# A hybrid decoder layer on one core: the rotation moves to VectorE, e's blocks later, scores in single banks, division on ScalarE

## The chip, the core and the metric

The kernel runs on one core of a Trainium2 chip. The core has a matrix engine (TensorE, PE in the profile), a vector engine (VectorE, DVE), an engine for activations (ScalarE, ACT), a general-purpose one (GpSimd, POOL) and SyncE (SP), which only issues transfers. Each works through its own queue in order and waits on semaphores for the others. Matrix products land in PSUM, which has eight banks of 2 KB a partition; everything else lives in SBUF. The metric is the device time of one execution in microseconds, the median over runs.

## The reference

One layer on a sequence of 512 tokens with 2048 features, all in 32-bit floats:

```
h = rms_norm(x, norm_gain);  z = h @ w_in
q, k, v, g_attn, c_b, c_c, c_h, g_conv = split(z)
q, k = partial_rope(rms_norm(q)), partial_rope(rms_norm(k))   # first 16 of 64 columns of a head turn
y_attn = sliding_window_attention(q, k, v, sinks) * silu(g_attn)
y_conv = c_b * short_conv(c_c * c_h) * silu(g_conv)
x = x + concat(y_attn, y_conv) @ w_out
gate = sigmoid(rms_norm(x) @ w_ple_gate + b)
e = rms_norm(p @ w_ple_proj)
x = x + gate * e
```

There are 16 query heads and 4 key heads of 64 columns. Attention looks back 128 tokens, so a block of 128 queries sees two blocks of keys (the first block sees one). The softmax has a learned sink in its denominator: probabilities are exp(scores - m) divided by (their sum + exp(sink - m)).

## The kernel before, in words

Each fp32 operand is split in two: a high half rounded to TensorE's fast 32-bit format (wh, hsh, made by a cast on ScalarE, L199) and the rest (wl, hsl, by a subtraction on VectorE, L200). A product is three matmuls, high by high, low by high, high by low. Large products are done in groups of 1024 output columns by a scheme of seven products of half blocks in place of eight, which is what `steps` lists; a step is 12 matmuls of 512 columns. `run_step` prepares the weights two steps ahead.

There are three parts. The first makes the keys, values and group 0 (the queries). The second, which most of the change touches, does what doesn't fit into groups. TensorE's queue is there written out by hand: `gemm_tile` runs 16 pairs of three matmuls (L701) for seven tiles of the short convolution's inputs, and after every second pair `tick` lets one piece of other work into the queue: transposes of keys (`make_k`), four blocks of `e_block` and sixteen units of `attention`, each for one key head j and one block n of 128 queries. `at(when, fn)` sets the tick. A unit turns its queries (`turn_q`, three ticks before), makes four heads' scores (L790, L791) into PSUM, takes the row minimum and mask on VectorE (L796), the exponential on ScalarE (L801), turns the probabilities (L816, five ticks later), splits them and multiplies by the values (L826, L827, two ticks after that). The other four engines' order in this part is set by a scheduler, from the order of the code and its own costs. In the first and third parts it is the order of the code.

An `e_block` multiplies p by 512 columns of w_ple_proj: 24 matmuls (L867) into four banks, one for each block of tokens. `take_e` then squares a bank on ScalarE with a row sum (L858), multiplies it by the gain on VectorE (L860) and stores it through GpSimd's queue (L861). Two of the four banks are the pair that attention's scores use (`ps_s`, one buffer of two banks), two are those of the turned probabilities (`ps_t`).

The rotation (`rope`) runs on GpSimd: four products with tables, one difference and one sum (L407 to L409), for each of four key blocks and four half-sets of queries. Query set (t, n) holds token blocks 2t and 2t+1 and heads 8n to 8n+7. Sets (0, 1) and (1, 1) are scaled and turned at the start of the second part, (0, 0) and (1, 0) inside it. Its scratch tile and most other short-lived tiles of this part come from one pool, `misc`, of eight buffers.

The third part runs groups 1 to 8. Group 4 is the attention's gate: its quarters z get silu (L992) on ScalarE; `normalise` (L1074) multiplies them on VectorE by `rs`, the reciprocals of the softmax sums; then TensorE turns them (L986) and VectorE multiplies the attention rows by them (L1083).

## Time and profile before

| | |
|---|---|
| median of 3 runs | 944.35 us (944.24 to 945.08) |
| profiled execution | 943.3 us, its span 941.5 us |
| TensorE busy | 915.0 us, 97% of the span |
| VectorE busy | 729.7 us, 78% |
| ScalarE busy | 532.5 us, 57% |
| GpSimd busy | 176.0 us, 19% |
| mean granted TensorE clock | 0.991 |
| second part | from 127.03 us; first scores at 184.95 us; last tile of the part at 294.35 us |

The span runs from the first to the last instruction; the execution's own time lies 1.8 us over it. A row of a timeline gives the start, the time to the end of the last of its instructions, the engine, the line, what is written from what, the shapes and, in brackets, how long the engine had been idle before and who ended that. Matmuls overlap, so the time between two starts says what one costs, not its own duration. A row of a group gives busy time in all, the mean of one in nanoseconds, and the idle time before them. In the row of a window the engines' busy times are followed by the TensorE clock that was granted as a share of full speed, the share of time that the transfer engines were busy, and GB/s.

### The profile page before, as it was taken

Reading aid. Unit: us, or ns where it says so; the run is one execution under the profiler, and the core shown is the slowest. Engines: PE = TensorE matmul, PEld = TensorE weight load, DVE = VectorE, ACT = ScalarE, POOL = GpSimd, SP = SyncE. Lnnn points to the kernel's source line nnn. Section 1 sums busy time; section 2 is a strip of 40 time slices with the busy share of each in tenths; the row PEclk is TensorE's granted clock in tenths of the full one; section 3 lists DMA queues with packets and bytes.
Section 4 is the critical chain, followed back from the end, with each engine's and each line's share of the span. In section 5 each row is a group of like instructions: output and inputs, shape, how many; then the busy total and the mean of one; then the engine's idle time right before and its main releaser. Section 6 shows DMA issues by size and latency. Waiting matters only on the chain.

```text
span 941.5 us, 12095 instructions
## 1 busy us (share of the span) xinstructions
PE 915.0 (97%) x4202; PEld 758.0 (81%) x4202; DVE 729.7 (78%) x1038; ACT 532.5 (57%) x855; POOL 176.0 (19%) x248
## 2 busy tenths in 40 slices
PE   9999997889999999999999999899999999999997
PEld 7888876678788888888888888788888888888885
DVE  5877976777873876877667768989678696999778
ACT  6767836477873443446344446455566676575453
POOL 4232196512222000100100120010221112001100
PEclk9999998999999999999999999999999999999999
DMA  8999434523557877435925887785997995578747
GB/s 296 361 291 325 164 109 165 196 79 79 101 95 198 311 222 233 121 112 173 239 80 160 275 215 234 224 219 139 261 332 223 225 287 158 135 226 271 185 134 213
DMA packets 69086, 189.83 MB, mean 202 GB/s; under 512 B 8097, under 2 KB 14561, under 8 KB 69025
## 3 DMA queue, kind: packets, MB, share of 16 engines
q1 hardware_dynamic: 47520, 131.09, 40.4%
q0 software_dynamic: 21360, 57.96, 27.5%
q8 instruction: 33, 0.54, 0.2%
q14 instruction: 29, 0.23, 0.1%
q10 hardware_dynamic: 144, 0.01, 0.0%
HBM read 159.67 MB, written 29.36 MB: 201 GB/s over the span
## 4 chain that ended last, share of the span: by engine, by line
PE 65%; DVE 3%; issue 1%; ACT 0%; DVEq 0%
PE psp L241 58%; PE pst L241 3%; PE pst L986 2%; PE pst L1339 1%; PE psg L701 1%; DVE wl L200 1%; DVE z L1239 1%; DVE wy L189 1%; DVE z L1074 0%; DVE form L200 0%; ACT z L992 0%; DVE z L1293 0%; DVE z L1224 0%; DVE z L1221 0%; DVE z L323 0%
## 5 line engine op out<-in xcount | busy, mean ns | idle before, releaser
L241 PE MATMUL psp<-wh,form 128*128 128x512 f32 x1280 | 395.2, 390 | 0.0
L241 PEld LDWEIGHTS psp<-wh,form 128*128 128x128 f32 x1280 | 239.3, 188 | 49.1
L241 PE MATMUL psp<-wl,form 128*128 128x512 f32 x640 | 249.2, 389 | 0.0
L200 DVE TENSOR_TENSOR wl<-wy,wh 128x1024 fp32r<-128x1024 f32 x108 | 131.7, 1222 | 53.7 <-ACT wh L199 53.0
L199 ACT CAST wh<-wy 128x1024 fp32r<-128x1024 f32 x108 | 113.5, 1051 | 101.2 <-PE psp L241 70.4
L241 PEld LDWEIGHTS psp<-wl,form 128*128 128x128 f32 x640 | 120.2, 188 | 25.0
L200 DVE TENSOR_TENSOR wl<-wx,wh 128x1024 fp32r<-128x1024 f32 x72 | 88.0, 1223 | 51.2 <-ACT wh L199 51.1
L241 PE MATMUL psp<-wh,hsh 128*128 128x512 f32 x304 | 119.3, 392 | 0.0
L241 PE MATMUL psp<-wh,hsl 128*128 128x512 f32 x304 | 118.7, 391 | 0.0
L241 PE MATMUL psp<-wl,hsh 128*128 128x512 f32 x304 | 118.7, 390 | 0.0
L199 ACT CAST wh<-wx 128x1024 fp32r<-128x1024 f32 x72 | 75.6, 1053 | 75.5 <-PE psp L241 51.9
L199 ACT CAST wh<-ws 128x1024 fp32r<-128x1024 f32 x72 | 75.9, 1054 | 73.7 <-PE psp L241 51.6
L200 DVE TENSOR_TENSOR wl<-ws,wh 128x1024 fp32r<-128x1024 f32 x72 | 88.1, 1223 | 28.6 <-ACT wh L199 28.5
L189 DVE TENSOR_TENSOR wy<-wy,ws 128x1024 f32<-128x1024 f32 x72 | 87.7, 1218 | 0.0
L241 PEld LDWEIGHTS psp<-wl,hsh 128*128 128x128 f32 x304 | 57.3, 189 | 12.2
L241 PEld LDWEIGHTS psp<-wh,hsh 128*128 128x128 f32 x304 | 57.4, 189 | 11.8
L241 PEld LDWEIGHTS psp<-wh,hsl 128*128 128x128 f32 x304 | 57.4, 189 | 11.8
L169 POOL DMA_DIRECT2D wy<-in_w_mid x16 | 14.1, 880 | 200.1 <-DVE wy L189 154.2
L701 PE MATMUL psg<-hsh,wh 128*128 128x512 f32 x112 | 46.3, 413 | 0.0
L200 DVE TENSOR_TENSOR wl<-raw,wh 128x1024 fp32r<-128x1024 f32 (+1 forms) x29 | 34.5, 1190 | 14.9 <-ACT wh L199 14.8
L701 PE MATMUL psg<-hsh,wl 128*128 128x512 f32 x112 | 44.0, 393 | 0.0
L701 PE MATMUL psg<-hsl,wh 128*128 128x512 f32 x112 | 43.8, 391 | 0.0
(217 smaller groups left out, 1345.0 us busy)
## 6 DMA issues: line engine op xcount, KB each, us to landing
ws<-in_w_mid SPq DMA_DIRECT2D x40, 512.0 KB, 4.3
wx<-in_w_mid SPq DMA_DIRECT2D x24, 512.0 KB, 3.6
wy<-in_w_mid SPq DMA_DIRECT2D x20, 512.0 KB, 5.3
h<-form POOLq DMA_DIRECT2D x32, 256.0 KB, 5.8
wy<-in_w_mid POOLq DMA_DIRECT2D x16, 512.0 KB, 8.5
raw<-in_w_in SPq DMA_DIRECT2D x16, 512.0 KB, 3.8
wx<-in_w_out SPq DMA_DIRECT2D x16, 512.0 KB, 6.7
ws<-in_w_out SPq DMA_DIRECT2D x16, 512.0 KB, 5.2
```

What stands on the lines that cost most here:

```text
L169: nc.gpsimd.dma_start(t, w[n, r, j, c], accum_op=ALU.add)
L189: tt(y, y, got[g, "s1" if f == 6 else "s0", c], op=ALU.add)
L199: nc.scalar.copy(h, src)
L200: tt(l, src, f32(h), op=ALU.subtract)
L241: nc.tensor.matmul(ps[t], a, w[:, i], start=start and first and i == 0 and n == 0, stop=last and i == 1 and n == 2, skip_group_check=not s ...
L701: nc.tensor.matmul(ps, w[:, k % 8], a, start=k == 0 and n == 0, stop=k == KT - 1 and n == 2)
L986: nc.tensor.transpose(pt[:, b], quads[b // 2][:, b % 2, f * P : (f + 1) * P], ident)
L1239: stt(z[:, b, cols], z[:, b, cols], column(r_e, t, b), ext[t, n][b][:, cols], op0=ALU.mult, op1=ALU.mult)
L1339: nc.tensor.matmul(ps, w[:, k % 8], a, start=k == 0 and n == 0, stop=k == KT - 1 and n == 2)
```

## The change

Four edits and some that follow from them.

- `rope` runs on VectorE (`tt`) and in two products over 16 columns in place of four over 8: the tables `turns` hold cosine and sine in the order in which each product takes them. Scratch tiles come from `misc` in the second part.
- The four blocks of e stand later in TensorE's queue: before the ninth, 17th, 21st and 25th pair of `gemm_tile` in place of the fifth, ninth, 17th and 21st. Each bank is taken after its own matmuls, and the first bank no longer waits for the second. The weights are loaded in the new order. `misc` has nine buffers.
- `ps_s` has two buffers of one bank each in place of one of two. A unit's four heads of scores use two tiles, which come free apart.
- In the gate, three of the four quarters are multiplied by `rs` on ScalarE, 8 activations of 64 columns at a time (one head of one token block each), in two halves at different steps. The last quarter stays on VectorE.
- The second half-sets of queries are squared, scaled and rotated at ticks 13 to 20 in place of 2 to 8. Two small constants are loaded first.

```diff
--- before.py
+++ after.py
...
@@ -389,24 +389,24 @@
     nc.gpsimd.tensor_tensor(kq_g, kq[:, 0:1], kq[:, 1:2], op=ALU.mult)
 
     half = ROT // 2
-    turns = [const.tile([P, 4, NB, half], F32, name=f"turn{i}") for i in range(2)]
+    turns = [const.tile([P, 2, NB, ROT], F32, name=f"turn{i}") for i in range(2)]
     for i in range(2):
-        for n, (what, part_) in enumerate(((0, 0), (1, 1), (0, 1), (1, 0))):
-            gain = rope_g[:, i, part_ * half : (part_ + 1) * half].unsqueeze(1).broadcast_to([P, NB, half])
-            nc.gpsimd.tensor_tensor(turns[i][:, n], trig[:, what], gain, op=ALU.mult)
-
-    work_tile = [itile]
-    def rope(z, which, blocks):
+        for n in range(2):
+            for p in range(2):
+                gain = rope_g[:, i, p * half : (p + 1) * half].unsqueeze(1).broadcast_to([P, NB, half])
+                nc.gpsimd.tensor_tensor(
+                    turns[i][:, n, :, p * half : (p + 1) * half], trig[:, (n + p) % 2], gain, op=ALU.mult
+                )
+
+    def rope(z, which, blocks, junk):
 
         nb, nh = z.shape[1], z.shape[2]
-        lo, hi = z[:, :, :, :half], z[:, :, :, half : ROT]
-        t = work_tile[0]("rope")[:, : 4 * nb * nh * half].rearrange("p (n b h d) -> p n b h d", n=4, b=nb, h=nh)
-        for n, src in enumerate((lo, hi, hi, lo)):
-            w = turns[which][:, n, blocks].unsqueeze(2).broadcast_to([P, nb, nh, half])
-            nc.gpsimd.tensor_tensor(t[:, n], src, w, op=ALU.mult)
-        nc.gpsimd.tensor_tensor(lo, t[:, 0], t[:, 1], op=ALU.subtract)
-        nc.gpsimd.tensor_tensor(hi, t[:, 2], t[:, 3], op=ALU.add)
+        t = junk("rope")[:, : 2 * nb * nh * ROT].rearrange("p (n b h d) -> p n b h d", n=2, b=nb, h=nh)
+        for n in range(2):
+            w = turns[which][:, n, blocks].unsqueeze(2).broadcast_to([P, nb, nh, ROT])
+            tt(t[:, n], z[:, :, :, :ROT], w, op=ALU.mult)
+        tt(z[:, :, :, :half], t[:, 0, :, :, :half], t[:, 0, :, :, half:], op=ALU.subtract)
+        tt(z[:, :, :, half:ROT], t[:, 1, :, :, :half], t[:, 1, :, :, half:], op=ALU.add)
 
 
     hs, kv_split = [], []
@@ -560,7 +560,7 @@
 
     def scale_k(b):
         tt(k_of(b), k_of(b), msk[:, b].unsqueeze(2).broadcast_to([P, NKV, HD]), op=ALU.mult)
-        rope(kv[b][:, : NKV * HD].rearrange("p (o h d) -> p o h d", o=1, d=HD), 1, slice(b, b + 1))
+        rope(kv[b][:, : NKV * HD].rearrange("p (o h d) -> p o h d", o=1, d=HD), 1, slice(b, b + 1), mtile)
 
     def q_of(t, n):
         return qs[t, n].rearrange("p b (h d) -> p b h d", d=HD)
@@ -578,7 +578,7 @@
             for b in range(2):
                 tt(z[:, b], z[:, b], ms[:, b].unsqueeze(2).broadcast_to([P, 8, HD]), op=ALU.mult)
 
-        return squares, lambda: head_rstd(ms, rx2_tok[:, blocks]), scale, lambda: rope(z, 0, blocks)
+        return squares, lambda: head_rstd(ms, rx2_tok[:, blocks]), scale, lambda: rope(z, 0, blocks, mtile)
 
     quarters(0, qs, 0)
     soon(after, 0, evict_kv)
@@ -587,8 +587,8 @@
     for j, s in enumerate((6, 6, 7, 7, 9, 9, 10, 10)):
         soon(after, s, form7, j)
 
-    jobs = [io["w_in"][TCC, 0], io["w_ple_proj"][0], io["w_ple_proj"][1], io["w_in"][TCC, 1], io["w_ple_proj"][2],
-            io["w_in"][TCH, 0], io["w_ple_proj"][3], io["w_in"][TCH, 1]]
+    jobs = [io["w_in"][TCC, 0], io["w_ple_proj"][0], io["w_in"][TCC, 1], io["w_ple_proj"][1],
+            io["w_in"][TCH, 0], io["w_ple_proj"][2], io["w_ple_proj"][3], io["w_in"][TCH, 1]]
     for i in range(1, 4):
         jobs += [io["w_in"][t + i, c] for t in (TCC, TCH) for c in range(2)]
     raws, splits, job = {}, {}, [0]
@@ -660,10 +660,10 @@
-    misc = second.enter_context(tc.tile_pool(name="misc", bufs=8, side="right", reuse_waits="tile"))
+    misc = second.enter_context(tc.tile_pool(name="misc", bufs=9, side="right", reuse_waits="tile"))
-    ps_s = second.enter_context(tc.tile_pool(name="ps_s", bufs=1, space=PSUM, reuse_waits="tile"))
+    ps_s = second.enter_context(tc.tile_pool(name="ps_s", bufs=2, space=PSUM, reuse_waits="tile"))
@@ -720,9 +719,9 @@
     scale_q(1, 1)
     for t in range(2):
         for b in range(2):
-            at(2 + t, lambda t=t, b=b: square_q(t, 0, b, mtile))
-        at(3 + t, lambda t=t: q_then[t, 0][0]())
-        at(7 + t, lambda t=t: scale_q(t, 0))
+            at(13 + t, lambda t=t, b=b: square_q(t, 0, b, mtile))
+        at(14 + t, lambda t=t: q_then[t, 0][0]())
+        at(19 + t, lambda t=t: scale_q(t, 0))
     mask = cw.tile([P, 2 * P], F32, name="mask", bufs=1)
     nc.gpsimd.dma_start(mask, io["mask"])
     vv = vvp.tile([P, NB, NKV, 2, HD], F32R, name="vv")
@@ -783,18 +782,19 @@
                 tt(st[oth, :, hf], pt[own], f32(st[own, :, hf]), op=ALU.subtract)
 
         def scores():
-            sc = ps_s.tile([P, 4, 2 * P], F32, name="pss")
+            sc = [ps_s.tile([P, 2, 2 * P], F32, name="pss") for _ in range(2)]
             ks = slice(n * P + lo - P, (n + 1) * P)
             for r in range(4):
                 q = cell["q"][:, r // 2, r % 2]
-                nc.tensor.matmul(sc[:, r, lo:], q, khh[j][:, ks], start=True, stop=False)
-                nc.tensor.matmul(sc[:, r, lo:], q, kll[j][:, ks], start=False, stop=True)
+                out = sc[r // 2][:, r % 2, lo:]
+                nc.tensor.matmul(out, q, khh[j][:, ks], start=True, stop=False)
+                nc.tensor.matmul(out, q, kll[j][:, ks], start=False, stop=True)
             t = ap.tile([P, 4, 2 * P], F32, name="prob")
             negm, sums, sk = (small.tile([P, 4], F32, name=x) for x in ("negm", "sums", "sk"))
             for r in range(4):
                 h = 4 * j + r
                 nc.vector.tensor_tensor_reduce(
-                    t[:, r, lo:], sc[:, r, lo:], mask[:, lo:], -(HD**-0.5), nsink[:, h : h + 1],
+                    t[:, r, lo:], sc[r // 2][:, r % 2, lo:], mask[:, lo:], -(HD**-0.5), nsink[:, h : h + 1],
                     ALU.add, ALU.min, negm[:, r : r + 1],
                 )
             for r in range(4):
@@ -850,8 +850,8 @@
         if n < 3:
             load_pg(n + 1)
         ws = next_job()
-        pair = ps_s.tile([P, 4, 2 * P], F32, name="pss").rearrange("p (t a) b -> p t (a b)", t=2)
-        banks = [pair[:, 0], pair[:, 1]] + [ps_t.tile([P, T], F32, name="pst") for _ in range(2)]
+        banks = [flat(ps_s.tile([P, 2, 2 * P], F32, name="pss")) for _ in range(2)]
+        banks += [ps_t.tile([P, T], F32, name="pst") for _ in range(2)]
 
         def take_e(t):
             e = mtile("e")
@@ -865,14 +865,14 @@
                 h, l = (a[:, k, t * P : (t + 1) * P] for a in pts)
                 for i, (a, w) in enumerate(((h, ws[0]), (l, ws[0]), (h, ws[1]))):
                     nc.tensor.matmul(banks[t], a, w[:, k], start=k == 0 and i == 0, stop=k == 1 and i == 2)
-            for i in {1: (0, 1), 2: (2,), 3: (3,)}.get(t, ()):
+            for i in (t,):
                 take_e(i)
 
     load_pg(0)
     order = [(j, n) for j in (2, 3, 0, 1) for n in range(NB)]
     for u, (j, n) in enumerate(order):
         attention(j, n, 13 + 34 * u // 15)
-    mids = {0: {4: lambda: e_block(0), 8: lambda: e_block(1)}, 1: {0: lambda: e_block(2), 4: lambda: e_block(3)}}
+    mids = {0: {8: lambda: e_block(0)}, 1: {k: lambda n=n: e_block(n) for n, k in ((1, 0), (2, 4), (3, 8))}}
 
 
     for i in range(4):
@@ -1062,21 +1062,28 @@
         s0, q = g * PER, {}
         quarters(g, q, s0)
         soon(after, s0 + 17, lambda: silu(q[0, 1], 0))
-        soon(after, s0 + 18, lambda: normalise(0, 1))
+        soon(after, s0 + 18, lambda: normalise(0, 1, 0))
+        soon(after, s0 + 19, lambda: normalise(0, 1, 1))
         soon(after, s0 + 21, lambda: silu(q[1, 1], 1))
-        soon(after, s0 + 22, lambda: normalise(1, 1))
+        soon(after, s0 + 21, lambda: normalise(1, 1, 0))
+        soon(after, s0 + 22, lambda: normalise(1, 1, 1))
         soon(after, s0 + 26, lambda: silu(q[0, 0], 0))
-        soon(after, s0 + 27, lambda: normalise(0, 0))
-
-        def normalise(t, n):
+        soon(after, s0 + 26, lambda: normalise(0, 0, 0))
+        soon(after, s0 + 27, lambda: normalise(0, 0, 1))
+
+        def normalise(t, n, h):
+
             for b in range(2):
-                z = q[t, n][:, b].rearrange("p (h d) -> p h d", d=HD)
-                tt(z, z, rs[:, 2 * t + b, 8 * n : 8 * n + 8].unsqueeze(2).broadcast_to([P, 8, HD]), op=ALU.mult)
+                for i in range(4 * h, 4 * h + 4):
+                    z = q[t, n][:, b, i * HD : (i + 1) * HD]
+                    nc.scalar.activation(z, z, AF.Copy, scale=rs[:, 2 * t + b, 8 * n + i : 8 * n + i + 1])
 
         def last():
             q[1, 0] = qtile("z")
             silu(q[1, 0], 1, psum[g, "a"])
-            normalise(1, 0)
+            for b in range(2):
+                z = q[1, 0][:, b].rearrange("p (h d) -> p h d", d=HD)
+                tt(z, z, rs[:, 2 + b, 0:8].unsqueeze(2).broadcast_to([P, 8, HD]), op=ALU.mult)
 
         def times(j):
             raw = pairs[id(mixf), j][0]
```

Where the scheduler and the code put the instructions now can be seen at three places. First VectorE at the start of the second part, before:

```order
L200 TENSOR_TENSOR wl<-raw,wh 128x1024
L710 COPY rb<-rx_tok 128x512
L562 TENSOR_TENSOR kv<-kv,msk 128x256 x4
L556 TENSOR_TENSOR msq<-msq,r_x 128x16 x2
L200 TENSOR_TENSOR wl<-raw,wh 128x1024
L579 TENSOR_TENSOR z<-z,msq 128x512 x4
L200 TENSOR_TENSOR wl<-raw,wh 128x1024
```

Here wl is the low half of the convolution's first weights, of e's first weights and of the convolution's second ones, kv a key and value block, msk and msq the heads' scales, z a query set. With the change the last rows ahead of the same cast of e's first weights, and that cast:

```order
L556 TENSOR_TENSOR msq<-msq,r_x 128x16 x2
L408 TENSOR_TENSOR kv<-rope 128x4x8
L409 TENSOR_TENSOR kv<-rope 128x4x8
L579 TENSOR_TENSOR z<-z,msq 128x512 x3
L407 TENSOR_TENSOR rope<-z,turn_225 128x256 x2
L579 TENSOR_TENSOR z<-z,msq 128x512
L408 TENSOR_TENSOR z<-rope 128x16x8
L409 TENSOR_TENSOR z<-rope 128x16x8
L407 TENSOR_TENSOR rope<-z,turn_225 128x256 x2
L200 TENSOR_TENSOR wl<-raw,wh 128x1024
```

In between stand the other rotations and scalings of the four key blocks. The cast of e's first weights moved behind all rotations of keys and one and a half of queries; it stood ahead of all of them.

Second VectorE from the second unit's last reduction to the third's first one. Before:

```order
L796 ISA negm 128x1
L887 TENSOR_TENSOR u<-psg,zc 128x512
L805 TENSOR_TENSOR sk<-attn_sinks,negm 128x4
L783 TENSOR_TENSOR st<-psm,st 64x2x128
L807 TENSOR_TENSOR sums<-sums,sk 128x4
L808 RECIPROCAL rs<-sums 128x4
L891 SCALAR_TENSOR_TENSOR yconv<-u,conv_w,yconv 128x512
L783 TENSOR_TENSOR st<-psm,st 64x2x128
L891 SCALAR_TENSOR_TENSOR yconv<-u,conv_w,yconv 128x512
L200 TENSOR_TENSOR wl<-raw,wh 128x1024
L796 ISA prob,negm<-pss,mask,nsink 128x256
```

and now:

```order
L796 ISA negm 128x1
L887 TENSOR_TENSOR u<-psg,zc 128x512
L805 TENSOR_TENSOR sk<-attn_sinks,negm 128x4
L556 TENSOR_TENSOR msq<-msq,r_x 128x16 x2
L200 TENSOR_TENSOR wl<-raw,wh 128x1024
L807 TENSOR_TENSOR sums<-sums,sk 128x4
L782 TENSOR_TENSOR st<-psm,st 64x2x128
L808 RECIPROCAL rs<-sums 128x4
L891 SCALAR_TENSOR_TENSOR yconv<-u,conv_w,yconv 128x512
L782 TENSOR_TENSOR st<-psm,st 64x2x128
L891 SCALAR_TENSOR_TENSOR yconv<-u,conv_w,yconv 128x512
L796 ISA prob,negm<-pss,mask,nsink 128x256
```

prob and negm are a head's masked scores and their row minimum, u and yconv the convolution's, st the turned queries. Two products of msq came in: the scales of the other query sets, which GpSimd's power has to give first; the cast wl moved ahead of the evictions st. Above and below these rows stand also four sums of squares (L548), four scalings (L579) and two rotations of those sets.

Third ScalarE in the gate, from the second quarter's silu (L992) on. Before:

```order
L992 ACTIVATE z<-z,r_x 128x512 x2
L199 CAST form<-raw 128x256
L199 CAST form<-g 128x256
L199 CAST wh<-wy 128x1024
L199 CAST form<-g 128x512
L199 CAST form<-g 128x256
L199 CAST wh<-ws_5409 128x1024
L199 CAST form<-raw 128x512
```

and now:

```order
L992 ACTIVATE z<-z,r_x 128x512 x2
L1079 ACTIVATE z<-z,rs 128x64 x8
L199 CAST form<-raw 128x256
L199 CAST form<-g 128x256
L199 CAST wh<-wy 128x1024
L1079 ACTIVATE z<-z,rs 128x64 x8
L199 CAST form<-g 128x512
L199 CAST form<-g 128x256
L199 CAST wh<-ws_5419 128x1024
L199 CAST form<-raw 128x512
```

wh is the high half of a step's weights, form that of an input block. Two groups of eight activations (L1079) stand now before the two weight casts that follow the silu.

5 lines of the change are left out of this document (2 added, 3 removed).

## The prediction

> **What bounds the kernel now.** I read the page's first lines, then the list of waits on TensorE, then the windows and the timeline of the stretches that the waits point to.
>
> ```profile
> span 941.5 us, 12095 instructions
> PE 915.0 (97%) x4202; PEld 758.0 (81%) x4202; DVE 729.7 (78%) x1038; ACT 532.5 (57%) x855; POOL 176.0 (19%) x248
> PE pss L867 <- DVE e L860: 11.8, 3, 6.0
> PE pss L790 <- DVE negm L796: 3.7, 3, 2.5
> PE pst L986 <- DVE z L1074: 2.4, 2, 2.1
> ```
>
> TensorE has work for 97% of the span, so the most that any schedule can win is the 26.5 us without it (941.5 - 915.0) and what its clock loses. The list says where most of it lies: three waits in the blocks of e (L867), three at the scores (L790), two at the transposes of group 4 (L986). All other TensorE work is untouched by the change. In the windows (engine busy times, then the granted clock, DMA share and GB/s) the clock stands behind the engines:
>
> ```profile
> 127.03:184.95 57.92, 46.15 (x191) 37.01 (x190) 37.91 (x62) 29.16 (x59) 39.49 (x67) 0.91 0.48 162
> 184.95:294.35 109.40, 105.07 (x584) 87.49 (x583) 81.06 (x256) 77.77 (x231) 29.53 (x36) 1.00 0.48 104
> 604.42:615.10 10.68, 8.27 (x34) 6.61 (x32) 10.68 (x15) 4.62 (x8) 1.14 (x2) 0.84 0.79 210
> 145.00:150.00 5.00, 4.99 (x12) 3.93 (x13) 2.90 (x5) 3.84 (x9) 2.58 (x2) 0.50 0.20 75
> 173.40:177.40 4.00, 3.98 (x11) 3.15 (x12) 2.10 (x4) 0.87 (x4) 1.63 (x3) 0.57 0.93 316
> 199.60:203.00 3.40, 3.37 (x21) 3.00 (x22) 1.75 (x6) 2.30 (x8) 0.00 (x0) 1.00 0.32 118
> 607.50:611.00 3.50, 3.48 (x11) 2.98 (x12) 3.50 (x5) 0.00 (x0) 0.00 (x0) 0.53 0.88 178
> ```
>
> After some waits the clock is halved (0.50, 0.57, 0.53), after another it isn't (1.00 from 199.60 on). The timeline of TensorE gives the waits themselves, and the chain of waits an undisturbed run of matmuls:
>
> ```profile
> 145.01 0.79 PE L867 MATMUL pss<-wh,ptsh 128*128 128x512 f32 x1 [6.01 <-DVE e L860]
> 160.35 0.50 PE L867 MATMUL pss<-wh,ptsh 128*128 128x512 f32 x1 [1.37 <-DVE e L860]
> 173.42 0.50 PE L867 MATMUL pss<-wh,ptsh 128*128 128x512 f32 x1 [4.39 <-DVE e L860]
> 184.95 0.22 PE L790 MATMUL pss<-khh,st 128*128 128x128 f32 x1
> 294.35 10.88 PE pst L1339 x48
> ```
>
> An undisturbed 128x512 matmul takes 0.227 us (48 in 10.88), at half clock about twice that, so the e stage costs more than its 11.8 us of waits. From 127.03, the first matmul of the convolution part, to the first score at 184.95 are 57.92 us. TensorE issues there 174 matmuls (78 of L701, 96 of L867) at 0.227, 39.5 us, and 16 small transposes at about 0.09, 1.4 us: 40.9. **17.0 us** of the stretch are waits and half clock.
>
> **Who makes e wait.** GpSimd does the rotation, and e's consumers stand behind it:
>
> ```profile
> L407 POOL TENSOR_TENSOR rope<-kv,turn 128x32 f32<-128x32 f32 x16 | 9.3, 610 | 0.3 <-DVE kv L562 0.3
> 127.03 6.32 POOL L407 TENSOR_TENSOR rope<-kv,turn 128x32 f32<-128x32 f32 x4 [0.29 <-DVE kv L562]
> 143.05 0.45 POOL L409 TENSOR_TENSOR z<-rope 128x128 f32<-128x128 f32 x1
> 140.96 0.69 DVE L860 TENSOR_TENSOR e<-pss,pg 128x512 f32<-128x512 f32 x1 [3.91 <-POOL z L409]
> ```
>
> The four k rotations and the first two of q hold GpSimd from 127.03 to 143.50; VectorE's first product of e waits 3.91 us for it, and TensorE's second block, whose banks those products free, waits 6.01. The products' stores also go through GpSimd:
>
> ```profile
> e<-e POOLq DMA_DIRECT2D x16, 256.0 KB, 2.9
> ```
>
> **The change, part by part.** (a) *Rotation on VectorE.* The prices come from VectorE's own rows at this place:
>
> ```profile
> 126.47 1.42 DVE L562 TENSOR_TENSOR kv<-kv,msk 128x256 f32<-128x256 f32 x4
> 127.81 0.33 DVE L556 TENSOR_TENSOR msq<-msq,r_x 128x16 f32<-128x16 f32 x2
> 128.06 1.21 DVE L200 TENSOR_TENSOR wl<-raw,wh 128x1024 fp32r<-128x1024 f32 x1
> 129.19 2.48 DVE L579 TENSOR_TENSOR z<-z,msq 128x512 f32<-128x512 f32 x4
> 131.60 1.21 DVE L200 TENSOR_TENSOR wl<-raw,wh 128x1024 fp32r<-128x1024 f32 x1
> ```
>
> From start to start these give 0.335 us for 256 columns, 0.125 for 16, 1.13 for 1024, 0.60 for 512. The rotation of k is 8 products of 64 columns and 8 sums of 32. No row has these sizes: at least 0.125 each, at most 0.335. I take 0.14 and 0.125, since the cost follows the columns: 2.1 us in place of GpSimd's 11. The two rotations of q are 4 products of 256 columns (1.34) and 4 sums of 128 (about 0.2 each). VectorE does them ahead of the low half of e's first weights. By the new order, from 126.47: four scalings of k 1.34, rotation 2.1, small ones 0.25, four scalings of q 2.4, four products 1.34, two sums 0.4, so that cast starts at 134.3 and lands 1.2 later, 135.5. TensorE gets there by 24 matmuls and 8 transposes, 5.45 + 0.72 after 127.03, and two matmuls: 133.65. A **new wait of 1.9 us**, between 1.6 (all small ones at 0.125) and 5.4 (all at 0.335).
>
> (b) *e's blocks later, taken part by part.* Blocks 1 to 3 come after the rotations. Between two blocks lie 12 or more matmuls, so a bank is asked for again some 7 us after its last matmul. TensorE fills a bank in 6 x 0.227 = 1.36, and VectorE's product of it takes 0.69, so the consumers keep its pace; if a store's landing (2.9) holds a buffer, the ninth one and the 7 us cover it, and without that cover a wait is like today's smallest, 1.37. I count no wait for blocks 1 to 3. The stage becomes 40.9 + 1.9 = 42.8, a **gain of 15.1 us** (11.6 with the long rotation, 15.4 with the short); the first score moves to 169.8.
>
> (c) *Scores in single banks, q's second half later.* The scores can follow after two of four reductions instead of four. But the squares, norms and rotations of the other half of q now stand among the first units of attention:
>
> ```profile
> 199.63 0.35 PE L790 MATMUL pss<-khh,st 128*128 128x256 f32 x1 [2.51 <-DVE negm L796]
> L548 DVE TENSOR_REDUCE msq<-sqq 128x8 f32<-128x512 f32 x8 | 5.3, 680 | 2.5 <-ACT sqq L547 2.5
> L796 DVE CUSTOM_DVE_ANT_0 prob<-pss,mask,nsink 128x256 f32<-128x256 f32 x48 | 20.3, 480 | 3.3 <-PE pst L816 3.1
> L305 POOL TENSOR_TENSOR msq<-msq,half_neg 128x16 f32<-128x16 f32 x4 | 12.6, 3140 | 4.4 <-DVE msq L300 4.4
> ```
>
> By the new order VectorE does, between the end of the first scores (170.7) and the third unit's reductions: the rest of e 0.4, four sums of squares 2.4, reductions 1.1 + 1.6, the evictions of q 4 x 0.35, u 0.6, a cast 1.13, two steps of the convolution 1.4, small ones 1.1. Before the cast it must also wait for two powers on GpSimd in a row at 3.14 us, which start near 174.6: 180.9. After them the cast, two evictions, two steps and small ones, 3.4, so the reductions start at 184.3 and two are done at 185.1. TensorE is ready for the fourth unit's scores at 181.7: a wait of 3.4 where 2.51 stands now. The four scalings (2.4) and two rotations (2 x 1.08) that come next push the fourth unit's work and the low halves of the second's probabilities, about 2 us of TensorE. With 0.7 for half clock and small waits I count 6.3 for the stage against 4.3 now (109.40 - 105.07 in its window): a **loss of 2.0**. Bounds: a gain of 4.3 if the early release takes all waits away, a loss of 9.6 if the added work passes to TensorE whole (2.4 + 2.4 + 2.2 + 0.9, and 1.7 for the powers).
>
> The Trainium skill, "TensorE: Matmul & The Clock Gate", Part 1, halves the clock after an idle window of about 3.4 us, free-running. The rows agree for 4.39 and 2.51, not for 607, where two waits of 2.12 and 0.30 sufficed. By it the 3.4 us wait is a toss-up, and the sum would be 0.7 less or 0.7 more.
>
> (d) *Division in the gate on ScalarE.* TensorE's rows at the transposes of group 4, then VectorE's and ScalarE's:
>
> ```profile
> 604.42 0.38 PE L986 MATMUL pst<-ident,z 128*128 128x128 f32 x2
> 606.92 0.30 PE L986 MATMUL pst<-ident,z 128*128 128x128 f32 x1 [2.12 <-DVE z L1074]
> 607.52 1.30 PE L986 MATMUL pst<-ident,z 128*128 128x128 f32 x5 [0.30 <-DVE z L1074]
> 615.10 1.03 PE L986 MATMUL pst<-ident,z 128*128 128x128 f32 x8
> 590.34 1.29 DVE L1074 TENSOR_TENSOR z<-z,rs 128x512 f32<-128x512 f32 x2
> 606.09 1.28 DVE L1074 TENSOR_TENSOR z<-z,rs 128x512 f32<-128x512 f32 x2
> 600.67 1.34 ACT L992 ACTIVATE z<-z,r_x 128x512 f32<-128x512 f32 x2 [3.35 <-DVE z L323]
> L801 ACT ACTIVATE prob<-prob,negm 128x128 f32<-128x128 f32 x16 | 6.2, 393 | 4.5 <-DVE negm L796 4.5
> L806 ACT ACTIVATE sk<-sk 128x4 f32<-128x4 f32 x16 | 3.2, 198 | 0.0
> ```
>
> From 604.42 to 615.10 TensorE does 8 transposes (0.87) and 24 matmuls (5.44); 4.4 us are lost to the wait for L1074 and half clock. VectorE is busy through the whole window (10.68 of 10.68), so the two pairs that leave it, 1.2 each, bring its queue 2.4 forward. ScalarE gets 48 activations of 64 columns with a per-row factor, 8 at a time, between the weight casts. Their rows lie between 0.20 (128x4) and 0.39 (128x128 with a per-row bias), 0.29 in the middle; two of L992 take 1.34 from start to end at some 0.72 each, so starts lie 0.1 closer than the durations. I take 0.21, 1.7 us for eight. The eight for the first transposes then end near 603, ahead of 604.42. Two eights delay the casts by 3.4 before the weights of the next two steps are due. So a **gain of 2.3**, what VectorE gives up; between -0.7 and 4.4.
>
> (e) Constants, loads of weights in another order, GpSimd's freed time: nothing. The constants are due at 127, over 100 us after they land, and each weight load still stands two jobs ahead of its cast. If that cover went, one load, 3.8 us to land.
>
> Sum: 941.5 - 15.1 + 2.0 - 2.3 = 926.1. The profiled execution took 943.3 for a span of 941.5, and the median is 944.35, 2.85 over the span: 926.1 + 2.85 = **929.0 us**.
>
> **The rivals.** *VectorE's queue in attention.* The loss of (c) at its upper bound, 9.6 instead of 2.0: 936.6. For it: the powers stand in VectorE's queue as waits. Against: it idles a fourth of the stage now. 17%.
>
> *e still waits.* Blocks 1 to 3 and the first scores each find a bank late by the smallest of today's waits, 1.37: 5.5 more, 934.5. For it: every product's buffer waits for a store. Against: the rotation that made it is gone. 13%.
>
> *Activations at the price of the row above, 0.39.* Eight take 3.1, the casts come 2.8 later than counted, (d) loses 0.7: 932.0. For it: a per-row factor. Against: half the columns, no sum read back. 14%. The Trainium skill, "ScalarE: Activation LUTs", Rules for kernel authors, budgets about 0.3 us per activation with such an operand and 0.83 ns for each element: an estimate of 0.35 for 64 columns. The same page gives plain multiplication to VectorE. No trace here shows the size.
>
> *Slower.* VectorE's row order puts a wait on another engine into every one of the 16 units, not only the first: at 1.3 us each, 21 us, (c) would cost more than (b) and (d) give, 948. It decides from 1.1 us a unit on. The added work is 0.5 a unit, so VectorE would have to stop for the rest. 4%.
>
> *It doesn't do what it says*: e's first cast comes at the long rotation's 5.4, TensorE waits at block 0 as long as it now does at block 1, and half clock follows for some ten matmuls: 929.0 + 3.5 + 2.3 = 934.8. 5%.
>
> **The numbers.** My own case has the other 47%, 925 to 933. The range goes from 924.5 (929.0 less 0.3 for the short rotation, 2.1 for all of group 4's loss, 2.0 for nothing lost in attention) to 938.5, two over the case of the queue in attention. Less than 0.2% is about what a measurement of this kernel cannot tell from none; every case but the slower one lies far below 944.35 - 1.9. So slower has 0.04, the same 0.02 (out of the last case, should the queue in attention come on top of it), faster 0.94.
>
> **What would show it.** Right: L867's waits shrink to one of about 2 us, at e's first block, for L200; the clock is 1.00 from 127 to the scores; they start near 170; L986 waits no more. Wrong: waits of L867 on L860 or a store; several waits of L790 or L826 over 3 us; rows of L1079 over 0.35 us and waits of L241 on L200 in group 4.

## The result, and the profile after

The changed kernel takes **933.7 us** (median, 931.94 to 934.14) where the kernel before took 944.48 in the same comparison: a ratio of 0.9881, with a 95% interval of 0.9864 to 0.9899. It is faster, as forecast, and the time lies in the stated range, but 4.7 us above the 929.0 that were predicted. The first lines of the profile's page, and then TensorE's waits in the second and third part (engine, line, what was waited for: us in total, times, longest):

```profile
span 932.4 us, 12106 instructions
PE 912.5 (98%) x4202; PEld 755.6 (81%) x4202; DVE 731.0 (78%) x1064; ACT 543.2 (58%) x903; POOL 150.5 (16%) x200
```

```profile
PE psm L777 <- DVE st L782: 2.6, 3, 1.0
PE pss L790 <- DVE negm L796: 2.5, 1, 2.5
PE psp L241 <- ACT wh L199: 2.1, 1, 2.1
PE psp L241 <- DVE wl L200: 2.0, 2, 1.9
PE psm L740 <- ACT rx L735: 1.4, 1, 1.4
PE pso L827 <- DVE ptl L200: 0.5, 1, 0.5
```

All waits of e's blocks (11.8 us before) and those of the gate's transposes (2.4) are gone. In their place stand a wait at the transposes of keys (L740), several small ones in attention (L777, L790, L827), and new ones at the weights of group 4 (L241). Three windows give the stages: e's from the first matmul of the convolution to the first scores, attention's from there to the first matmul of the second part's last tile (L1339 before, L1346 now), and everything from that matmul on (the engines' busy times, then the granted clock, DMA share, GB/s). Two more windows show the time behind two of the waits.

```profile
127.00:169.99 42.99, 41.59 (x192) 34.10 (x191) 34.78 (x71) 27.41 (x55) 8.18 (x15) 1.00 0.67 219
169.99:282.32 112.33, 106.62 (x583) 89.12 (x582) 88.57 (x279) 78.93 (x236) 35.50 (x39) 0.98 0.45 100
282.32:932.40 650.08, 639.60 (x2881) 528.91 (x2879) 505.58 (x564) 345.83 (x465) 67.21 (x82) 1.00 0.71 207
185.53:189.53 4.00, 3.99 (x15) 3.40 (x16) 3.81 (x14) 2.09 (x10) 0.00 (x0) 0.59 0.18 68
613.00:617.00 4.00, 3.96 (x10) 2.73 (x11) 2.37 (x3) 4.00 (x12) 0.00 (x0) 0.59 1.05 279
```

Before, the three stages took 57.92, 109.24 and 647.31 us (from the starts 127.03, 184.95 and 294.19 in TensorE's timeline to the span's end at 941.5); now they take 42.99, 112.33 and 650.08. So e's stage gained **14.9 us**, attention lost **3.1**, and the rest, in which only the gate of group 4 was changed, lost **2.8**. Together that is the 9.1 us between the two spans. The four largest waits that are left, in TensorE's timeline:

```profile
134.48 0.66 PE L740 MATMUL psm<-ident,kv 128*128 128x128 f32 x4 [1.40 <-ACT rx L735]
185.53 0.36 PE L790 MATMUL pss<-khh,st 128*128 128x256 f32 x1 [2.54 <-DVE negm L796]
596.08 0.50 PE L241 MATMUL psp<-wl,hsh 128*128 128x512 f32 x1 [1.87 <-DVE wl L200]
613.00 1.22 PE L241 MATMUL psp<-wh,form 128*128 128x512 f32 x2 [2.09 <-ACT wh L199]
```

### The profile page after: what moved, and what is told of

Read it like the earlier page. It is cut to its first block, busy times and chain, and to the rows that moved or that the text cites. A ratio compares the mean times of both kernels' runs of the same rounds, so it can differ in the third digit from the quotient of the medians.

```text
span 932.4 us, 12106 instructions
## 1 busy us (share of the span) xinstructions
PE 912.5 (98%) x4202; PEld 755.6 (81%) x4202; DVE 731.0 (78%) x1064; ACT 543.2 (58%) x903; POOL 150.5 (16%) x200
## 4 chain that ended last, share of the span: by engine, by line
PE 64%; DVE 3%; ACT 1%; DMA 1%; issue 1%; SPq 0%; DVEq 0%
PE psp L241 57%; PE pst L241 4%; PE pst L986 1%; DMA e<-e 1%; PE pst L1346 1%; PE psg L700 1%; DVE wl L200 1%; ACT z L1079 1%; DVE form L200 0%; DVE wy L189 0%; ACT z L992 0%; DVE raw L1090 0%; ACT wh L199 0%; DVE z L323 0%; ACT form L199 0%
## 5 line engine op out<-in xcount | busy, mean ns | idle before, releaser
L241 PE MATMUL psp<-wh,form 128*128 128x512 f32 x1280 | 396.3, 391 | 2.1 <-ACT wh L199 2.1
L241 PEld LDWEIGHTS psp<-wh,form 128*128 128x128 f32 x1280 | 240.0, 188 | 51.7 <-ACT wh L199 2.5
L241 PE MATMUL psp<-wl,form 128*128 128x512 f32 x640 | 249.8, 390 | 0.0
L200 DVE TENSOR_TENSOR wl<-wy,wh 128x1024 fp32r<-128x1024 f32 x108 | 131.7, 1222 | 54.6 <-ACT wh L199 53.8
L241 PEld LDWEIGHTS psp<-wl,form 128*128 128x128 f32 x640 | 120.4, 188 | 25.8 <-DVE wl L200 0.8
L200 DVE TENSOR_TENSOR wl<-wx,wh 128x1024 fp32r<-128x1024 f32 x72 | 88.0, 1223 | 51.1 <-ACT wh L199 51.0
L241 PE MATMUL psp<-wl,hsh 128*128 128x512 f32 x304 | 118.7, 390 | 2.0 <-DVE wl L200 2.0
L241 PE MATMUL psp<-wh,hsh 128*128 128x512 f32 x304 | 118.8, 391 | 0.0
L241 PE MATMUL psp<-wh,hsl 128*128 128x512 f32 x304 | 118.3, 389 | 0.0
L200 DVE TENSOR_TENSOR wl<-ws,wh 128x1024 fp32r<-128x1024 f32 x72 | 88.1, 1223 | 29.0 <-ACT wh L199 28.8
L241 PEld LDWEIGHTS psp<-wl,hsh 128*128 128x128 f32 x304 | 57.1, 188 | 14.9 <-DVE wl L200 2.9
L241 PEld LDWEIGHTS psp<-wh,hsl 128*128 128x128 f32 x304 | 57.1, 188 | 11.8
L241 PEld LDWEIGHTS psp<-wh,hsh 128*128 128x128 f32 x304 | 57.1, 188 | 11.7 <-ACT wh L199 0.2
L200 DVE TENSOR_TENSOR wl<-raw,wh 128x1024 fp32r<-128x1024 f32 (+1 forms) x29 | 34.4, 1187 | 15.2 <-ACT wh L199 15.0
```

The costliest lines, as they stand in the source:

```text
L200: tt(l, src, f32(h), op=ALU.subtract)
L241: nc.tensor.matmul(ps[t], a, w[:, i], start=start and first and i == 0 and n == 0, stop=last and i == 1 and n == 2, skip_group_check=not s ...
```

## The experiments

Most change one thing in the changed kernel; the second starts from the kernel before, and the eleventh and twelfth put several changes together. For each run the table gives its median, the median of the kernel before measured beside it, the ratio with its interval, and the three stages of its profiled execution, read from the starts of the convolution's first matmul, of the first scores (L790) and of the last tile's first matmul in TensorE's timeline, and from the span. Undoing is marked with "back".

| kernel | us | before | ratio | e | attention | rest |
|---|---|---|---|---|---|---|
| before | | | | 57.92 | 109.24 | 647.31 |
| the change | 933.70 | 944.48 | 0.9881 (0.9864 to 0.9899) | 42.99 | 112.33 | 650.08 |
| 1 gate back on VectorE | 931.94 | 944.58 | 0.9863 (0.9849 to 0.9877) | 43.02 | 112.02 | 647.27 |
| 2 before, gate alone | 946.68 | 944.58 | 1.0021 (1.0012 to 1.0029) | 58.52 | 109.21 | 649.44 |
| 3 e's places back | 936.71 | 944.58 | 0.9914 (0.9895 to 0.9932) | 48.87 | 109.53 | 649.22 |
| 4 rotation back on GpSimd | 936.79 | 944.58 | 0.9916 (0.9902 to 0.9931) | 47.59 | 110.16 | 649.08 |
| 5 another bank for rb | 933.21 | 944.04 | 0.9886 (0.9871 to 0.9901) | 42.94 | 112.27 | 649.69 |
| 6 pair of banks back | 950.42 | 944.04 | 1.0068 (1.0056 to 1.0081) | 59.04 | 113.18 | 649.18 |
| 7 q's sums into e | 931.56 | 944.04 | 0.9866 (0.9853 to 0.9880) | 43.02 | 109.64 | 649.22 |
| 8 q's second half later | 930.40 | 944.04 | 0.9857 (0.9844 to 0.9871) | 42.99 | 109.51 | 649.21 |
| 9 pair back, taken together | 934.90 | 944.38 | 0.9900 (0.9883 to 0.9917) | 43.06 | 113.29 | 649.22 |
| 10 gate mixed | 929.41 | 944.38 | 0.9833 (0.9819 to 0.9848) | 42.99 | 112.16 | 645.69 |
| 11 = 8 and 10 | 926.78 | 944.38 | 0.9807 (0.9793 to 0.9821) | 42.99 | 109.51 | 645.40 |
| 12 = 11, no wait in e | 925.14 | 944.22 | 0.9797 (0.9784 to 0.9810) | 41.39 | 109.47 | 645.30 |

### 1 and 2: what the gate's division costs

The first puts the division back on VectorE in the changed kernel; the second moves only the division in the kernel before.

```diff
-        soon(after, s0 + 18, lambda: normalise(0, 1, 0))
-        soon(after, s0 + 19, lambda: normalise(0, 1, 1))
+        soon(after, s0 + 18, lambda: normalise(0, 1))
...
-                    nc.scalar.activation(z, z, AF.Copy, scale=rs[:, 2 * t + b, 8 * n + i : 8 * n + i + 1])
+                tt(z, z, rs[:, 2 * t + b, 8 * n : 8 * n + 8].unsqueeze(2).broadcast_to([P, 8, HD]), op=ALU.mult)
```

> The changed kernel (933.7 us) with the gate's division back on VectorE in all four quarters, as before. Theory A (the 48 activations of 64 columns stand ahead of weight casts on ScalarE, and TensorE's new waits at 596 and 613 us, 2.0 and 2.1 us for casts and low halves, come from that): those waits go, the wait of the gate's transposes for L1074 of 2.1 us comes back, and 2.9 us are won, the amount by which the stretch from 586 us to the end's constant distance is longer than before: 930.8 us. Theory B (the prediction's: VectorE's 2.4 us are the gain and the new waits have another cause, such as transfers that collide because everything is 12 us earlier): the waits at the weights stay and the transposes' wait is added, 933.7 + 2.3 = 936.0 us.

> The kernel before (944.4 us) with only the gate's division moved to ScalarE for three quarters. Theory A (activations delay the weight casts): 2.9 us slower, 947.3 us, with waits of L241 for casts (L199) or low halves (L200) in group 4. Theory B (VectorE's time is the gain): 2.3 us faster, 942.1 us. If the time is 944.4, the loss in the changed kernel needs the other edits.

Measured: 931.94 us for the first, 1.8 us won where theory A expected 2.9. Its interval overlaps that of the changed kernel, so the medians alone would not settle it, but the rest of the kernel took 647.27 us, where every kernel with the division moved as in the change took 649.1 to 650.1, and the waits went as theory A says. For the second the ratio settles it: 1.0021 (1.0012 to 1.0029), **slower** by the division alone, 2.1 us where 2.9 were expected. The waits of TensorE in group 4, first with the gate back, then in the kernel before with the gate alone:

```profile
PE pst L986 <- DVE z L1074: 2.4, 2, 2.1
```

```profile
PE psp L241 <- DVE wl L200: 2.4, 2, 1.9
PE psp L241 <- ACT wh L199: 1.0, 1, 1.0
```

The old wait and the new ones take each other's place, and the new ones cost more. Why is read in the changed kernel from ScalarE's and then VectorE's timeline ahead of the wait at 596.08:

```profile
588.63 1.34 ACT L992 ACTIVATE z<-z,r_x 128x512 f32<-128x512 f32 x2 [3.05 <-DVE z L323]
589.87 2.01 ACT L1079 ACTIVATE z<-z,rs 128x64 f32<-128x64 f32 x8
591.78 0.39 ACT L199 CAST form<-raw 128x256 fp32r<-128x256 f32 x1
592.20 0.43 DVE L200 TENSOR_TENSOR form<-raw,form 128x256 fp32r<-128x256 f32 x1 [2.47 <-ACT form L199]
593.68 1.22 DVE L189 TENSOR_TENSOR wy<-wy,ws 128x1024 f32<-128x1024 f32 x1
594.81 1.22 DVE L200 TENSOR_TENSOR wl<-wy,wh 128x1024 fp32r<-128x1024 f32 x1
```

Eight activations take 1.91 us from start to start (589.87 to 591.78), and the cast of the next input block stands behind them. VectorE stops 2.47 us for that cast, its low half of the weights lands at 596.03, and TensorE, which asked for it 1.87 us earlier, starts at 596.08. So VectorE did get its time back, and spent it standing still. At 613.00 the same happens with the first eight of the third quarter (609.39 to 611.31): VectorE stops 2.95 us for the cast behind them, and TensorE waits 2.09 us for the next high half. The other four groups of eight cost TensorE next to nothing: no wait behind the two of the first quarter (577.14 and 580.31), 0.15 us behind the second one of the second quarter (593.33), none behind the last.

The transposes did get their gain. From the first to the second transposes of the gate the change takes 9.21 us, where the kernel before took 10.68, although the wait of 1.87 us lies in between; what is lost lies between the second and the third, first in the kernel before, then both stretches in the change:

```profile
615.10:629.60 14.50, 14.50 (x70) 12.09 (x69) 12.83 (x19) 8.10 (x12) 2.36 (x3) 1.00 1.00 272
```

```profile
592.49:601.70 9.21, 7.19 (x33) 5.20 (x32) 9.18 (x14) 7.50 (x16) 0.87 (x1) 1.00 0.73 212
601.70:620.31 18.61, 16.48 (x69) 12.85 (x68) 13.54 (x20) 12.10 (x29) 2.59 (x3) 0.91 0.88 235
```

Of the 4.1 us, 2.1 are time without work; most of the others go with the granted clock, 0.91 in this stretch for 1.00.

### 3 and 4: the rotation's engine and the place of e's blocks

The third has e's blocks and the order of the loads of the kernel before, the fourth the rotation in its new form on GpSimd.

```diff
-    mids = {0: {8: lambda: e_block(0)}, 1: {k: lambda n=n: e_block(n) for n, k in ((1, 0), (2, 4), (3, 8))}}
+    mids = {0: {4: lambda: e_block(0), 8: lambda: e_block(1)}, 1: {0: lambda: e_block(2), 4: lambda: e_block(3)}}
```

```diff
-            tt(t[:, n], z[:, :, :, :ROT], w, op=ALU.mult)
+            nc.gpsimd.tensor_tensor(t[:, n], z[:, :, :, :ROT], w, op=ALU.mult)
...
```

> The changed kernel with e's four blocks and the order of the weight loads back at the old places (before the fifth, ninth, 17th and 21st pair); the rotation stays on VectorE, the banks are taken one by one. Theory A (the rotation's engine made e's blocks wait; the place only has to leave room for the rotation): one larger wait at the first block for the low half of its weights, cast at about 135.2 us where TensorE asks for it at 130.6: 4.6 us in place of 1.4, some 2 us of half clock behind it, no waits at the other blocks: 933.7 + 3.2 + 2 = 939 us. Theory B (the later place is what ended the waits): the second to fourth blocks wait for the first products (L860) again, 1.4 to 6.0 us each as before: 943 us or more.

> The changed kernel with the rotation, in its new form of two products, on GpSimd again; e's blocks stay late. Theory A (rotation's engine decides): GpSimd has the four rotations of keys done at about 137 us, so the first transposes of keys, reached at 132.9 us, wait some 4 us instead of 1.4, and with half clock behind that 933.7 + 2.7 + 2 = 938 us; e's later blocks wait no more than now, since their products no longer need what GpSimd holds. Theory B (the later place alone suffices): 933.7 us. Theory C (GpSimd holds VectorE's products and the stores as before): waits at L867 for L860 of several us, 942 us or more.

Measured: 936.71 and 936.79 us, 2.3 and 1.2 below what theory A gave, at least 5 below the 942 and more of the third's theory B and the fourth's theory C, and 3.1 above the 933.7 of the fourth's theory B. Each part alone keeps most of the gain in e's stage (9.1 and 10.3 of 14.9 us), and neither alone all of it. With e early there is one wait, where and as large as expected; with the rotation on GpSimd the waits are at the transposes of keys:

```profile
135.22 0.79 PE L867 MATMUL pss<-wl,ptsh 128*128 128x512 f32 x1 [4.46 <-DVE wl L200]
```

```profile
PE psm L740 <- POOL kv L409: 3.7, 4, 1.6
```

The first and the third pair of products in GpSimd's timeline, and VectorE's work beside the first:

```profile
127.56 6.04 POOL L407 TENSOR_TENSOR rope<-kv,turn 128x64 f32<-128x64 f32 x2 [0.30 <-DVE kv L562]
136.13 0.58 POOL L407 TENSOR_TENSOR rope<-kv,turn 128x64 f32<-128x64 f32 x2
129.80 2.49 DVE L579 TENSOR_TENSOR z<-z,msq 128x512 f32<-128x512 f32 x4
132.21 1.22 DVE L200 TENSOR_TENSOR wl<-raw,wh 128x1024 fp32r<-128x1024 f32 x1
```

The total came out better than theory A's because attention took 109.5 and 110.2 us instead of 112.3, and the rest 0.9 and 1.0 less. In the third, VectorE comes to attention with less undone: its first sum of squares (L548) starts 1.5 us before the first scores (174.32 for 175.85), in the change 1.4 after them (171.43 for 169.99), and it never stops for GpSimd's powers. There a part of what e's stage wins in the change is paid back in attention. In the fourth that is not the cause: the powers start as long after the first scores as in the change (4.7 us), VectorE stops as long for them (1.39 us for 1.37), and the fourth unit's scores wait 2.58 us for 2.54. What is gone are two later waits, of 0.97 and 0.53 us; the rotations of q's second half, ahead of them in VectorE's queue in the change, run here on GpSimd; that this is the reason is read from the two queues and not tested by itself (VectorE's row, then GpSimd's):

```profile
185.73 0.18 DVE L556 TENSOR_TENSOR msq<-msq,r_x 128x16 f32<-128x16 f32 x1 [1.39 <-POOL msq L305]
193.43 1.43 POOL L407 TENSOR_TENSOR rope<-z,turn 128x256 f32<-128x256 f32 x2 [2.76 <-DVE rs L808]
```

### 5: what is late next in e's stage

```diff
     def rx2_rows():
-        pb = ps_m.tile([P, T], F32, name="psm")
+        pb = flat(ps_o.tile([P, 4, P], F32, name="pso"))
```

> The changed kernel with the transposes of rb (L734) in another PSUM bank than the transposes of keys (L740), so that these no longer wait 1.40 us for ScalarE's copy of the first. Theory A (the prediction's cast is next late behind it: the low half of e's first weights ends at 135.2 us, and TensorE then asks for it at about 133.7): the wait only moves, to L867 for L200, 1.3 to 1.6 us, and the first scores stay at 170.0: 933.7 us. Theory B (the cast had no part): no wait is left before e, first scores at 168.6, 932.3 us.

Measured: 933.21 us, e's stage 42.94. Theory A: the wait only moved, from L740 to the third matmul of e's first block, for the cast that the prediction had named.

```profile
135.65 0.50 PE L867 MATMUL pss<-wl,ptsh 128*128 128x512 f32 x1 [1.24 <-DVE wl L200]
```

### 6 and 9: single banks

The sixth gives the scores and e's first two banks one buffer of two banks again; the ninth also takes these two banks of e together, as before.

```diff
-            sc = [ps_s.tile([P, 2, 2 * P], F32, name="pss") for _ in range(2)]
+            pr = ps_s.tile([P, 4, 2 * P], F32, name="pss"); sc = [pr[:, 2 * i : 2 * i + 2] for i in range(2)]
...
-            for i in (t,):
+            for i in {1: (0, 1), 2: (2,), 3: (3,)}.get(t, ()):
```

> The changed kernel with one PSUM buffer of two banks for the scores and for two of e's banks, as before, in place of two buffers of one. Theory A (single banks matter little: a unit's scores wait for four reductions of 0.4 us in place of two): the wait of 2.54 us at the fourth unit's scores grows by 0.8, 934.5 us, and no block of e waits. Theory B (they are what keeps e's blocks from waiting): L867 waits for L860 again at the second to fourth block, 1.4 us or more each, 938 us or more.

> As the run with the pair of banks in one buffer, but e's first two banks are taken together after the second bank's matmuls, as before the change. In that run each of e's four blocks waited once, always at its seventh matmul, the first that writes the second bank, for the product of the first bank. Theory A (two banks in one buffer cost only when they are taken apart; the rest of single banks' worth is the 0.85 us that the fourth unit's scores waited longer, 3.39 for 2.54): no wait of L867 for L860, 933.7 + 0.85 = 934.5 us. Theory B (single banks are what lets e's next block start in time): a wait at the first matmul of the second to fourth block, 1.4 us or more each, 938 us or more.

Measured: 950.42 us for the sixth, 16 us worse than expected of theory A and worse than the kernel before. But the waits are not where theory B puts them, at the start of a block: each of the four is at a block's seventh matmul, the first into the second bank.

```profile
136.02 0.39 PE L867 MATMUL pss<-wl,ptsh 128*128 128x512 f32 x1
140.08 0.79 PE L867 MATMUL pss<-wh,ptsh 128*128 128x512 f32 x1 [3.67 <-DVE e L860]
158.12 0.50 PE L867 MATMUL pss<-wh,ptsh 128*128 128x512 f32 x1 [3.94 <-DVE e L860]
169.93 0.50 PE L867 MATMUL pss<-wh,ptsh 128*128 128x512 f32 x1 [1.50 <-DVE e L860]
180.38 0.50 PE L867 MATMUL pss<-wh,ptsh 128*128 128x512 f32 x1 [1.73 <-DVE e L860]
```

The first row is the sixth matmul of block 0; behind the first two waits the clock is at half (0.50 and 0.60 over 4 us), so the stage loses 16 us and not only the 10.8 of the waits. The two banks are one tile, and the place of the waits shows that the program orders accesses by whole tiles: once the first bank is to be read, the second bank's matmuls wait for that read. Taken together after the second bank (the ninth), the same pair costs no wait of e, and 934.90 us in all; its interval overlaps the changed kernel's. What is left of single banks is the fourth unit's wait, 3.33 us for 2.54, as theory A said:

```profile
186.05 0.36 PE L790 MATMUL pss<-khh,st 128*128 128x256 f32 x1 [3.33 <-DVE negm L796]
```

So taking e part by part needs the single banks, and with them is worth about nothing here; the scores gain the 0.8 us at this wait. Of the attention stage, 113.29 us with the pair and 112.33 without in one profiled execution each, single banks change the waits more than that: those of L790 for L796 fall from 4.5 to 2.5 us, those of the query transposes (L777) grow from 0.5 to 2.6.

### 7 and 8: where q's second half stands

```diff
-            at(13 + t, lambda t=t, b=b: square_q(t, 0, b, mtile))
-        at(14 + t, lambda t=t: q_then[t, 0][0]())
-        at(19 + t, lambda t=t: scale_q(t, 0))
+            at(17 + t, lambda t=t, b=b: square_q(t, 0, b, mtile))
+        at(18 + t, lambda t=t: q_then[t, 0][0]())
+        at(25 + t, lambda t=t: scale_q(t, 0))
```

(The seventh has 9, 10 and 19.)

> The changed kernel with the second half of q squared and normed at ticks 9 to 11 in place of 13 to 15 (the scaling and rotation stay at 19 and 20), so that the two powers on GpSimd (3.1 us each) and the sums fall into e's third block. Theory A (the wait of 2.54 us at the fourth unit's scores comes from VectorE stopping 1.37 us for these powers and from the sums beside them): it falls below 1 us, the attention stage from 112.3 to about 109.5 us, e's blocks give back at most 1 us: 931 to 932 us. Theory B (VectorE is short over both stages together, the wait only moves into e): 933.7 us, with a wait of L867 for L860 or L200 in e's third or fourth block.

> The changed kernel with the second half of q squared at ticks 17 and 18 and scaled and rotated at 25 and 26, in place of 13 to 20: behind the first four units of attention. Theory A (what stands between the second and third unit makes the wait of 2.54 us): that wait goes, those of the later units stay under 1 us, 931 us. Theory B (the first units are late anyway because VectorE comes out of e with work undone, and the sums only move the wait): one wait of 2 us or more at a later unit's scores or values, 933.7 us.

Measured: 931.56 and 930.40 us, attention 109.6 and 109.5 us for 112.3, e's stage unchanged. Theory A in both by the totals, though in the seventh a wait of 1.88 us is left at the fourth unit, more than the 1 us that was expected, and in the eighth four of 0.96 to 1.16. More than half of the gain is clock: TensorE is busy for 104.9 and 105.0 us of the stage in place of 106.6 for the same matmuls, since the clock stays at 1.00 behind these waits where it fell to 0.59 in the change; the time without work falls by only 0.9 and 1.2. In the changed kernel the stop is seen in VectorE's queue, and the two powers in GpSimd's:

```profile
174.70 5.80 POOL L305 TENSOR_TENSOR msq<-msq,half_neg 128x16 f32<-128x16 f32 x2 [2.35 <-DVE msq L300]
180.53 0.18 DVE L556 TENSOR_TENSOR msq<-msq,r_x 128x16 f32<-128x16 f32 x1 [1.37 <-POOL msq L305]
```

### 10 to 12: a version that beats both

The tenth leaves on ScalarE all of the first quarter and half of the second, that half two steps later; the rest of the division is VectorE's (`divide` is the product on VectorE over some of the heads).

```diff
-        soon(after, s0 + 21, lambda: normalise(1, 1, 0))
-        soon(after, s0 + 22, lambda: normalise(1, 1, 1))
+        soon(after, s0 + 21, lambda: divide(1, 1, 0, 4))
+        soon(after, s0 + 24, lambda: normalise(1, 1, 1))
         soon(after, s0 + 26, lambda: silu(q[0, 0], 0))
-        soon(after, s0 + 26, lambda: normalise(0, 0, 0))
-        soon(after, s0 + 27, lambda: normalise(0, 0, 1))
+        soon(after, s0 + 27, lambda: divide(0, 0, 0, 8))
```

> The changed kernel with the gate's division on ScalarE only where it cost no wait: all of the first quarter (16 activations, as now) and the second half of the second quarter (8, two steps later); the other half of the second quarter and the whole third go back to VectorE. From the end of the second part to the end of the span it took 647.3 us before and with the division all on VectorE (4.4 of them lost at the transposes), 649.2 to 650.1 with it on ScalarE. Theory A (casts behind the activations are the loss, and what VectorE gives up is worth its 1.8 us at the transposes): neither wait is left or both are under 0.5 us: 643 to 645 us, in all 927.5 to 929.5. Theory B (any activations there delay a weight cast by as much as they free): 647 us or more, 931 us or more.

> The mixed division and the second half of q at ticks 17, 18, 25 and 26 together. If the two gains add up (3.3 from the later q as measured, 4.2 to 6.2 from the gate): 924 to 926 us. If the gate's gain is not there: 930.4 us. If they share a cause, such as the granted clock of the whole run: 928 us.

The twelfth has, beside both, the bank of the fifth and one line moved:

```diff
-    scale_q(1, 1)
+    at(4, lambda: scale_q(1, 1))
```

> The version with the mixed division and the later q (926.8 us), the transposes of rb in another bank, and the second rotated half-set of q (block set 1) put at tick 4, which brings the low half of e's first weights forward in VectorE's queue. Theory A (the wait before e is held by two things that stand one behind the other, the bank and that cast; only both together take it away): no wait at L740 or at e's first block, the first scores 1.4 us earlier, 925.4 us. Theory B (VectorE is short in the whole stage, and what is moved back makes a later block of e or the first scores wait): 926.8 us, with a wait of L867 for L860 or of L777 for L782 that the changed kernel doesn't have.

Measured: 929.41, 926.78 and **925.14 us**, the last at a ratio of 0.9797 (0.9784 to 0.9810). The tenth's rest of 645.69 us lies between the two theories: the 1.87 and 2.09 us waits went, 0.2, 0.2 and 0.5 for low halves stayed. The eleventh wins 6.9 us over the changed kernel where 3.3 and 4.3 would add up to 7.6, so the two add up but for a little. In the twelfth e's stage has no wait left: moving the bank alone (the fifth) had uncovered the cast, and both together take the wait away. The cast alone was not moved in any run; that the bank's wait would then have stayed is read from its coming first.

```profile
span 923.4 us, 12082 instructions
```

and two of its windows:

```profile
127.24:168.63 41.39, 41.39 (x192) 34.18 (x190) 34.81 (x71) 27.14 (x55) 8.14 (x15) 1.00 0.66 227
588.25:595.62 7.37, 6.96 (x34) 5.18 (x33) 7.37 (x10) 6.05 (x15) 0.85 (x1) 1.00 0.72 175
```

TensorE is busy for all 41.39 us of the first window. The second, from the first to the second transposes of the gate, took 10.68 before and 9.21 in the change.

## Why the prediction was right, and where it was not

Summed over the terms: the span was forecast at 926.1 and measured at 932.4, 6.3 us more. Of these e's stage has 0.2, attention 1.1, the gate 5.1. The median lies 1.3 over the profiled span, not 2.85 as taken over from the kernel before, which hides 1.5 of it: that is luck. At 933.7 the time lies just above the 925 to 933 of the prediction's own case, inside a range that was drawn wide for a rival that did not come.

**(a), (b) e's stage: right, the number by luck.** Forecast 42.8, measured 42.99. The two parts of the forecast were off by as much in opposite directions: the stage without a wait takes 41.39 (the twelfth run), 0.5 more than the 40.9 counted, and the wait was 1.40, 0.5 less than the 1.9. VectorE's prices held: two products of 256 columns took 0.67 from start to start, sums of 128 columns 0.20, and the low half of e's first weights ended at 135.2 where 135.5 was forecast.

```profile
133.33 0.76 DVE L407 TENSOR_TENSOR rope<-z,turn 128x256 f32<-128x256 f32 x2
134.00 1.22 DVE L200 TENSOR_TENSOR wl<-raw,wh 128x1024 fp32r<-128x1024 f32 x1
135.44 0.40 PE L867 MATMUL pss<-wl,ptsh 128*128 128x512 f32 x1
```

The wait of 1.9 us that this cast was to cause appeared as 1.40 at another place: the transposes of keys share a bank with those of rb, whose copy stood in ScalarE's queue behind a cast (132.90) and began at 133.85. That wait came first and covered the cast, which ended 0.2 us before its matmul; the fifth run uncovers it. No wait in blocks 1 to 3 was right too. VectorE did wait twice for a store of e (1.50 and 1.22 us), and TensorE did not feel it. That the ninth buffer and the 7 us between blocks are the reason is argued; no run has eight buffers.

**(c) Attention: mechanism right, its terms mis-sized.** The two powers were forecast to end at 180.9 and ended at 180.5; the fourth unit's scores were forecast to start at 185.1 and started at 185.53, after a wait of 2.54 us. The terms as written, 3.4, about 2 and 0.7, add up to 6.1 and not the 6.3 that was counted. Against them the stage has 5.7 us without work (112.33 - 106.62): 2.54 at the fourth unit where 3.4 stood, and 3.1 in four small waits (0.63, 0.97 and 0.97 at L777, 0.53 at L827) where about 2 was counted. Too small is above all the term "With 0.7 for half clock and small waits": the clock fell to 0.59 behind the 2.54 us, where it had stayed at 1.00 behind the 2.51 us of the kernel before, and TensorE is busy 1.7 us longer for the same matmuls (106.62 for 104.91). So the first term was 0.9 too large, and the other two together measured 4.8 where 2.7 stood. The stage lost 3.1 us, not 2.0. Runs 7 and 8 show that the added work and not the single banks made the loss: with it elsewhere the stage takes 109.5, near the 109.24 before. It takes the early first scores as well: in run 3 the work stands where the change has it, the scores come 5.9 us later, and the stage takes 109.5 too.

**(d) The gate: wrong, and of the other sign.** A gain of 2.3 was forecast, and the stage lost 2.8 (1.8 to 2.8 over the runs that kept it). The step that failed is "Two eights delay the casts by 3.4 before the weights of the next two steps are due". The price was nearly right (0.24 from start to start for 0.21), but in two places there was no slack: ScalarE, though busy for only 26.1 of the 40 us from 586 on, gets its silu late from VectorE (the 3.05 us of its row at 588.63; the prediction's own row of the kernel before has 3.35), and what follows in its queue is already awaited. Of the six groups of eight, 1.91 us each, two went into TensorE's waits whole, as 1.87 and 2.09 us. VectorE's time did give a gain, 1.5 us up to the second transposes; between these and the third 4.1 were lost. The waits of L241 on L200 in group 4 that came are one of the signs by which the prediction said it would be wrong. The rival "Activations at the price of the row above" had the mechanism and asked for the wrong condition; it needed no higher price. The Trainium skill, "ScalarE: Activation LUTs", Rules for kernel authors, gives plain multiplication to VectorE, and its budget led to the prediction's estimate of 0.35 us for one activation. The rows agree with both: 0.33 us is the duration of one, and the division was cheaper on VectorE until it was put where ScalarE had time.

```profile
L1079 ACT ACTIVATE z<-z,rs x48: 332/333/345, 577.1 to 614.5; 128x64 f32<-128x64 f32 x48
```

**The rivals.** VectorE's queue in attention cost 3.1 us, not 9.6. e's waits did not come back. The slower case and the case that the change doesn't do what it says did not happen. Two of them, e's waits at 934.5 and the activations' price at 932.0, lie near the measured time, for reasons that the rows don't show: there is no wait of L867, and the price is 0.24 and not 0.39.
